# Weights of 32 experts loaded in 8 KB runs, inputs' columns permuted where they are made, the first low parts made behind the first gather, DFT tables loaded one by one

## The chip, the cores and the metric

One Trainium2 chip, one of its cores. The metric is the time of one execution in device microseconds, the median of several runs; lower is better. The profile shows one execution by engine: PE (TensorE), DVE (VectorE), ACT (ScalarE), POOL (GpSimd), SP (SyncE, which issues the DMAs of the weights).

## The reference

A backbone of two layers over 1024 tokens of 1024 columns (D), with 256 context tokens read by the first. Layer 0 mixes tokens by grouped-query attention, layer 1 by a Fourier transform; both are followed by a mixture of experts:

```python
h = _modulate(x, norm_ffn[i], sh2, sc2)          # rms norm, gain, shift, scale
lg = xt @ w_rg + b_rg                            # 4 groups of 8 experts: the best group,
le_sel = take_along_axis(xt @ w_re + b_re, ...)  # then its 2 best experts
gate = p_grp[:, None] * softmax(top_l)
# each expert e, over the tokens routed to it:
yb = (silu(xb @ w1[e]) * (xb @ w3[e])) @ w2[e]   # 1024 -> 512 -> 1024, float32
x = x + g2 * segment_sum(yb * gate)
```

w1 and w3 of an expert are 1024x512, w2 is 512x1024, all float32: 6 MiB an expert, 192 MiB a layer, each byte read once.

## The kernel before

**A MoE layer.** `phase_moe` (called once per layer) goes over the 32 experts. For each, POOL gathers up to 104 (CAP) rows of the normed input from a table H in DRAM with an indirect DMA (L1264, into one of several `xg` buffers). `xin` transposes the rows on PE and splits them into a high part `xh` (ACT) and a low part `xl` (DVE, L1277). Each weight comes in two pieces of 1 MiB, each piece as two quarters of 128x1024; `quarter` makes of a quarter its rounded part `wh` (ACT, L1203) and the rest `wl = t - wh` (DVE, L1205; one of twelve on POOL, and the first five of a layer, `POOL_FIRST`). Three matmuls per tile (L192 to L194) join them. `hidden` multiplies silu(h1) by h3 into `gg` (DVE, L1295), `gT` transposes it, and after w2 DVE scales the result by the gate (L1315), and POOL scatter-adds it to the stream Xs (L1316).

**Order of contraction.** A contraction over 1024 rows is done in 8 matmuls of 128 rows, one per partition. `load_piece` (L168 to L177) reads a piece as "(k p) n": partition p holds the rows p, 128 + p, ... of the piece, so each row is a run of its own in DRAM: 2 KB for w1 and w3, 4 KB for w2.

**Buffers.** Raw pieces go where space is free: `raw` tiles, a pair of tiles `qs`, the place of the two old row tiles (`X`, from the stage before, whole or a pair), and the tiles `wh`/`wl` of the old weights (`place`, `g.raws`). `feed` issues a load (SP queue) whenever a buffer is free. At most `NHELD` = 11 pieces of a layer are loaded before its first gather; `resume` makes SP's further loads wait until that gather has landed. `split(n)` makes the quarters ready, three ahead.

**Ahead of a layer's first gather.** The stage before (the attention's output projection in layer 0, the Fourier stage in layer 1) goes over 8 row tiles; `route_half` (L935) multiplies a tile's halves by the gain, `route_transpose` makes `hT` for the router and updates `h` (L963) for H, `route_part` picks experts and positions for some tiles (small DVE operations, L1047 to L1111). The last two tiles end the chain: `slot_index` compares positions (one-hots, L1156), PE turns them into row numbers `idx` (L1163), and POOL gathers. In layer 0 `vectors` also loads rows norm_mix, mod (`G2`, `V`) and nine tables for the DFT of the next layer, on SP, ahead of the held weights' last, and makes `V` (DVE, L1333).

Of the kernel before, what the change touches and what calls it, by code (L numbers as in the profile page):

```python
# [15 lines left out]
OP = mybir.AluOpType  # L16
# [46 lines left out]
NSP_EARLY = 3  # L63
NRAW = 3
NHELD = 11
DROP1, DROP2 = (10, (3, 4)), (27, 2)
POOL_FIRST, POOL_LAST = 5, 380
ORDER = (0, 4, 1, 5, 6, 7, 2, 3)
# [60 lines left out]


def rsqrt(g, pool, dst, src, scale, shape, tag, pw=False):
# [12 lines left out]
    nc.vector.tensor_mul(dst, dst, a)  # L144
# [22 lines left out]

def load_piece(g, src, k, eng=None):  # L168

    t = raw_tile(g)  # L170
    eng = eng or g.nc.sync
    src = src.rearrange("(k p) n -> p k n", p=P)
    ts = t if isinstance(t, list) else [t]
    k //= len(ts)
    for i, v in enumerate(ts):
        eng.dma_start(v.rearrange("p (k n) -> p k n", k=k), src[:, k * i:k * i + k])
    return t  # L177
# [622 lines left out]
def phase_wo(g):  # L800
# [4 lines left out]
    with ExitStack() as st:  # L805
# [4 lines left out]
        with ExitStack() as sw:  # L810
# [33 lines left out]
            for t in range(NT):  # L844
# [47 lines left out]
                if t == NT - 2:  # L892
                    sf.close()
                    mo.open_vectors("right")
        place(NT - 2)
        mo.open_weights("right")
        route_transpose(g, r, NT - 1, rwk, pt_)
        with tc.issue_after(r.last):
            mo.vectors()
        mo.begin_weights(r)  # L900
        route_logits(g, r, 3, rwk, pt_)
# [6 lines left out]
def route_setup(g, mo, one, wk):  # L908
# [3 lines left out]
    r.B2 = one.tile([P, D], F32, name="B2")  # L912
    nf = wk.tile([P, D], F32, name="h")
    bcast_row(g, r.A2, g.mod[l][0:1, 4 * D:5 * D])
    bcast_row(g, nf, a["norm_ffn"][l:l + 1])
    bcast_row(g, r.B2, g.mod[l][0:1, 3 * D:4 * D])
# [3 lines left out]
    nc.gpsimd.dma_start(r.W[:, :, 0:NG], a["moe_w_rg"][l].rearrange("(k p) n -> p k n", p=P))  # L920
    nc.gpsimd.dma_start(r.W[:, :, NG:NG + NE], a["moe_w_re"][l].rearrange("(k p) n -> p k n", p=P))
    r.bias = one.tile([P, NG + NE], F32, name="br")
# [32 lines left out]
def route_transpose(g, r, t, wk, pt_):  # L955
# [6 lines left out]
    transposed(g, u, r.hT[b][:, :, i], pt_, t in ACT_COPY[r.l])  # L962
    nc.vector.scalar_tensor_tensor(u, u, r.rs[t], r.B2, OP.mult, OP.add)  # L963
    r.last = nc.sync.dma_start(r.H[t * P:(t + 1) * P], u).ins
    r.order.append(t)
# [180 lines left out]
def slot_index(g, m, wk, pp, n, posm, val, tag):  # L1146
# [4 lines left out]
    for e in range(n):  # L1151
        oh = wk.tile([P, NT, CAP], BF, name="oneh")
        pe = posm(e)
# [15 lines left out]
class Moe:  # L1169


    def __init__(self, g, l):
# [11 lines left out]
        self.limit = len(self.order)  # L1184
        self.raw, self.sp = {}, {}
        self.stores = []
# [35 lines left out]
    def resume(self, ins):  # L1222

        g, n = self.g, self.nl
        self.limit = len(self.order)
        cur = g.nc.cur_bb.bb.instructions
        last = cur[-1]
        self.feed()
        for i in cur[next(k for k in range(len(cur) - 1, -1, -1) if cur[k] is last) + 1:]:
            g.tc.add_manual_dep(i, ins.name, mybir.DependencyInfo(mybir.DependencyClass.Sync, mybir.DependencyReason.DATA),  # L1230
                                reason="after the rows' gather")

    def begin_weights(self, r):
        self.limit = min(self.limit, NHELD)
        with self.g.tc.issue_after(r.last):
            self.use(4 - NRAW)
        with self.g.tc.issue_after(self.g.pow):
            self.split(NSP_EARLY - 1)

# [14 lines left out]
    def load(self, which, e, i, eng=None):  # L1254
# [35 lines left out]
    def hidden(self, h1, h3):  # L1290
# [70 lines left out]
def phase_moe(g, mo, after=None, fin=None):  # L1361
# [4 lines left out]
    with mo.st as st:  # L1366
# [26 lines left out]
        for e in range(NE + 1):  # L1393
# [29 lines left out]
            if e < NE:  # L1423
# [118 lines left out]

def dft_table(g, pool, name, tag=None):
# [4 lines left out]
    g.table = g.nc.sync.dma_start(t.bitcast(F32), src).ins  # L1548
    return t
# [513 lines left out]
```

## Time and profile before

| | us |
|---|---|
| median of 3 runs | 2396.41 |
| lowest and highest run | 2396.03, 2400.58 |
| the profiled execution, its own time | 2399.03 |
| its span, first to last instruction | 2396.9 |

The profile belongs to the execution of 2399.03 us, 2.6 above the median; 2.1 us of it lie outside the span. Over the span PE is busy 90%, DVE 80%, ACT 56% and POOL 42%, and the DMA engines move 614.22 MB. Rows of the profile give a start and a duration in us, the engine, the line of the kernel, the operation, the tile written and the tiles read.

### The profile page before, as it was taken

The numbers are of one execution on the slowest core, as the hardware profiler recorded it, in microseconds if no ns is written. First come the engines' busy times: TensorE is split into PE (matmuls) and PEld (weight loads), VectorE is DVE, ScalarE is ACT, GpSimd is POOL, SyncE is SP. The second block draws the span as 40 slices with busy tenths as digits, with TensorE's granted clock in tenths as the row PEclk, the third lists the DMA queues.
The fourth block names the chain that finished last, engine by engine and source line by source line (L and its number), as shares of the span: only waits on it lengthen the run. The fifth ranks groups of instructions, "written<-read, shape, count | busy, mean of one in ns | idle before, by whom it ended". The sixth has DMA issues, their size and how long they took to land.

```text
span 2396.9 us, 29626 instructions
## 1 busy us (share of the span) xinstructions
PE 2158.6 (90%) x10250; PEld 1427.3 (60%) x10250; DVE 1914.0 (80%) x2812; ACT 1334.2 (56%) x1741; POOL 1012.5 (42%) x562
## 2 busy tenths in 40 slices
PE   6898999999999858999999999689599999999994
PEld 3676444444445646677676667457377776666662
DVE  4868566666667897999889888666899988888895
ACT  5733433433443236777766667443387766666674
POOL 3322666666668643334333332433424433222232
PEclk8999999999999978999999999879699999999997
DMA  8544533533334769999999999745699999999996
GB/s 305 189 155 131 176 114 116 189 115 131 101 116 166 264 229 299 348 337 329 333 342 333 340 336 349 253 179 192 225 320 326 332 335 334 337 329 334 338 352 220
DMA packets 257878, 614.22 MB, mean 256 GB/s; under 512 B 26896, under 2 KB 43896, under 8 KB 251516
## 3 DMA queue, kind: packets, MB, share of 16 engines
q1 hardware_dynamic: 215676, 547.39, 65.4%
q0 software_dynamic: 24576, 54.40, 9.1%
q10 hardware_dynamic: 17472, 10.49, 1.4%
q8 instruction: 82, 1.34, 0.2%
q14 instruction: 72, 0.59, 0.1%
HBM read 559.57 MB, written 78.44 MB: 266 GB/s over the span
## 4 chain that ended last, share of the span: by engine, by line
PE 38%; DMA 29%; DVE 22%; issue 6%; ACT 3%; POOL 1%; SPq 0%; POOLq 0%; ACTq 0%; DVEq 0%
DVE wl L1205 9%; DMA raw<-in_moe_w_dram 9%; DMA wh<-in_moe_w_dram 7%; PE po L650 6%; DMA wl<-in_moe_w_dram 5%; PE sm L547 4%; PE st L644 3%; PE st L645 3%; DMA X<-in_moe_w_dram 2%; PE h L193 2%; PE h L194 2%; PE h L192 2%; PE mm L192 2%; PE mm L193 2%; PE mm L194 2%
## 5 line engine op out<-in xcount | busy, mean ns | idle before, releaser
L193 PE MATMUL h<-wl,xh 128*104 128x512 f32 x1024 | 414.5, 405 | 25.3 <-DVE wl L1205 15.0
L192 PE MATMUL h<-wh,xh 128*104 128x512 f32 x1024 | 413.5, 404 | 7.6 <-ACT wh L1203 7.5
L194 PE MATMUL h<-wh,xl 128*104 128x512 f32 x1024 | 407.7, 398 | 0.0
L670 POOL TENSOR_TENSOR acc<-acc,pe 128x1024 f32<-128x1024 f32 x125 | 298.7, 2389 | 96.5 <-ACT pe L659 94.0
L548 DVE TENSOR_REDUCE m<-sm 128x1 f32<-128x512 f32 x360 | 206.4, 592 | 136.2 <-PE sm L547 134.6
L659 ACT ACTIVATE pe<-st 128x1024 f32<-128x1024 f32 x160 | 163.9, 1025 | 261.5 <-PE st L645 258.8
L1203 ACT CAST wh<-raw 128x1024 fp32r<-128x1024 f32 x196 | 199.3, 1053 | 67.2 <-DMA raw<-in_moe_w_dram 44.3
L193 PEld LDWEIGHTS h<-wl,xh 128*104 128x104 f32 x1024 | 174.6, 171 | 103.5 <-DVE wl L1205 26.3
L1205 DVE TENSOR_TENSOR wl<-raw,wh 128x1024 fp32r<-128x1024 f32 x175 | 212.0, 1250 | 29.5 <-ACT wh L1203 28.8
L1264 POOL DMA_INDIRECT xg<-H,idx x64 | 103.5, 1617 | 302.8 <-PE pt L1275 273.4
L1203 ACT CAST wh<-wh 128x1024 fp32r<-128x1024 f32 x180 | 184.0, 1051 | 79.2 <-DMA wh<-in_moe_w_dram 48.2
L1205 DVE TENSOR_TENSOR wl<-wl,wh 128x1024 fp32r<-128x1024 f32 x163 | 205.2, 1286 | 20.3 <-ACT wh L1203 20.0
L1205 DVE TENSOR_TENSOR wl<-wh 128x1024 fp32r<-128x1024 f32 x157 | 191.8, 1246 | 33.8 <-ACT wh L1203 30.6
L192 PEld LDWEIGHTS h<-wh,xh 128*104 128x104 f32 x1024 | 174.7, 171 | 73.9 <-ACT wh L1203 13.0
L1203 ACT CAST wh<-wl 128x1024 fp32r<-128x1024 f32 x172 | 176.0, 1052 | 67.0 <-DMA wl<-in_moe_w_dram 41.3
L194 PEld LDWEIGHTS h<-wh,xl 128*104 128x104 f32 x1024 | 174.3, 170 | 59.2
L193 PE MATMUL py<-wl,gh 128*104 128x512 f32 x512 | 203.6, 398 | 0.5 <-POOL wl L1205 0.2
L194 PE MATMUL py<-wh,gl 128*104 128x512 f32 x512 | 201.2, 395 | 0.7 <-DVE gl L1306 0.7
L192 PE MATMUL py<-wh,gh 128*104 128x512 f32 x512 | 197.1, 402 | 2.0 <-ACT gh L1305 1.8
L650 PE MATMUL po<-pe,V 128*64 128x512 f32 x640 | 174.6, 624 | 0.4 <-ACT pe L659 0.4
L1316 POOL DMA_INDIRECT Xs<-y,idx x64 | 148.9, 2326 | 39.2 <-DVE y L1315 12.1
L1203 ACT CAST wh<-X 128x1024 fp32r<-128x1024 f32 x124 | 129.0, 1054 | 47.1 <-PE h L194 32.4
(569 smaller groups left out, 4496.0 us busy)
## 6 DMA issues: line engine op xcount, KB each, us to landing
raw<-in_moe_w_dram SPq DMA_DIRECT2D x98, 1024.0 KB
wh<-in_moe_w_dram SPq DMA_DIRECT2D x90, 1024.0 KB
wl<-in_moe_w_dram SPq DMA_DIRECT2D x86, 1024.0 KB
qs<-in_moe_w_dram SPq DMA_DIRECT2D x96, 512.0 KB
raw<-in_w_mod_dram SPq DMA_DIRECT2D x43, 1024.0 KB
X<-in_moe_w_dram SPq DMA_DIRECT2D x37, 1024.0 KB
X<-in_moe_w_dram SPq DMA_DIRECT2D x50, 512.0 KB
QS<-qst ACTq DMA_DIRECT2D x32, 256.0 KB
```

The lines of the kernel that those rows point to most:

```text
L192: nc.tensor.matmul(out, lh, wh, start=start, stop=False)
L193: nc.tensor.matmul(out, lh, wl, start=False, stop=False)
L194: nc.tensor.matmul(out, ll, wh, start=False, stop=stop)
L547: nc.tensor.matmul(ps[:, :kn], qs[:, h, qt * P:(qt + 1) * P], g.KS[:, g4, k0:k0 + kn], start=True, stop=True)
L548: nc.vector.reduce_max(m3[:, h, qt, b:b + 1], ps[:, :kn], axis=AX.X)
L650: nc.tensor.matmul(po[64 * h:64 * h + 64], g.V[:, kt, g4 * HD:(g4 + 1) * HD], pe[:, h], start=(kt == 0), stop=(kt == NTA - 1))
L659: nc.scalar.activation(pe, ps, AF.Exp, scale=SCALE)
L670: eng.tensor_add(acc, acc, pe)
L1203: nc.scalar.copy(h, t)
L1205: i = (nc.gpsimd if pool else nc.vector).tensor_sub(l, t, h)
L1264: self.last = self.g.nc.gpsimd.indirect_dma_start(out=xg, out_offset=None, in_=self.H if src is None else src, in_offset=bass.IndirectOffs ...
L1316: return y, lambda: nc.gpsimd.indirect_dma_start(out=self.X, out_offset=bass.IndirectOffsetOnAxis(ap=idx, axis=0), in_=y, in_offset=None, ...
```

## The change

1. A piece is read as "(p k) n": partition p holds k rows that follow each other, and a piece that goes into one tile is read in runs of 8 KB (4 KB into a pair of tiles). For the products to fit, the columns of what the weights are multiplied by are permuted: `route_half` writes `h`, and `hidden` writes `gg`, with their columns in the order in which the transposes then give them (the inner loop of the output strides 128 elements, 512 bytes). B2 is permuted by a POOL copy, the router's weights are loaded in the new order with four DMAs in place of two.
2. The first five low parts (`NLATE`) are made by DVE, after a POOL memset (`behind`) that is issued behind the first gather; the one-hots of experts 1 to 3 come after them, and the `prep` of expert 0 after X[1]. `oneh` has 3 buffers.
3. Layer 0: 2 raw buffers in place of 3, the last `place` moved, the last store of H on ACT's queue; `G2`, `V` and the product `V` move up into the loop over tiles; the nine tables load one per expert, for experts 8 to 16; G2's second row after expert 0. Layer 1's final norm comes after expert 6.

```diff
-NRAW = 3
+NRAW = (2, 3)
 NHELD = 11
 DROP1, DROP2 = (10, (3, 4)), (27, 2)
...
-def load_piece(g, src, k, eng=None):
+def load_piece(g, src, k, eng=None, order="(k p) n -> p k n"):
 
     t = raw_tile(g)
     eng = eng or g.nc.sync
-    src = src.rearrange("(k p) n -> p k n", p=P)
+    src = src.rearrange(order, p=P)
     ts = t if isinstance(t, list) else [t]
     k //= len(ts)
     for i, v in enumerate(ts):
-        eng.dma_start(v.rearrange("p (k n) -> p k n", k=k), src[:, k * i:k * i + k])
+        g.piece = eng.dma_start(v.rearrange("p (k n) -> p k n", k=k), src[:, k * i:k * i + k]).ins
     return t
 
 
...
-        place(NT - 2)
+                    mo.next_norm()
         mo.open_weights("right")
         route_transpose(g, r, NT - 1, rwk, pt_)
-        with tc.issue_after(r.last):
-            mo.vectors()
-        mo.begin_weights(r)
+        mo.begin_weights(r, lambda: place(NT - 2))
         route_logits(g, r, 3, rwk, pt_)
         with tc.issue_after(g.lt):
             mo.split(NSP - 1)
...
+def by_weights(t):
+
+    return t.rearrange("t (q j p) -> t q p j", q=2, j=4)
+
+
 def route_half(g, r, t, x1, n, wk):
 
     if n == 0:
         r.u[t] = wk.tile([P, D], F32, name="h")
     ns = slice(n * 512, n * 512 + 512)
-    g.nc.vector.tensor_mul(r.u[t][:, ns], x1[:, ns], r.A2[:, ns])
+    x, a2 = (v[:, ns].rearrange("t (p j) -> t p j", j=4) for v in (x1, r.A2))
+    g.nc.vector.tensor_mul(by_weights(r.u[t])[:, n], x, a2)
 
 
 def route_stats(g, r, t, x1, wk, junk):
...
-        pool = self.ns < POOL_FIRST if self.ns < 12 else self.ns % 12 == 9 and (self.ns < POOL_LAST or not self.l)
+        if self.ns < NLATE:
+            self.late.append((l, t, h))
+            return h, l
...
+    def finish_late(self):
+
+        for l, t, h in self.late:
+            self.vsub = self.g.nc.vector.tensor_sub(l, t, h).ins
+        self.late = []
+        self.feed()
+
...
-        nc.vector.tensor_mul(gg, s_, h3)
+
+        nc.vector.tensor_mul(gg.rearrange("t (i j p) -> t i p j", i=2, j=2), s_.rearrange("t (i p j) -> t i p j", i=2, j=2),
+                             h3.rearrange("t (i p j) -> t i p j", i=2, j=2))
...
+    def next_norm(self):
+
         g, nc = self.g, self.g.nc
         if self.l:
-            bcast_row(g, self.V, g.a["final_norm"].rearrange("(o d) -> o d", o=1), nc.sync)
-        else:
-            bcast_row(g, self.G2, g.a["norm_mix"][1:2], nc.sync)
-            bcast_row(g, self.V, g.mod[1][0:1, D:2 * D], nc.sync)
-            nc.vector.scalar_tensor_tensor(self.V, self.V, 1.0, self.G2, OP.add, OP.mult)
-            t = self.tab = {}
-            for n in ("cch", "ccl", "csh", "csl", "ce", "ci", "ca", "alt", "c0"):
-                t[n] = dft_table(g, self.vec, n)
-        bcast_row(g, self.G2, g.mod[self.l][0:1, 5 * D:6 * D], nc.sync)
+            with g.tc.issue_after(self.piece):
+                bcast_row(g, self.V, g.a["final_norm"].rearrange("(o d) -> o d", o=1), nc.sync)
+            return
+        bcast_row(g, self.G2, g.a["norm_mix"][1:2], nc.sync)
+        bcast_row(g, self.V, g.mod[1][0:1, D:2 * D], nc.sync)
+        nc.vector.scalar_tensor_tensor(self.V, self.V, 1.0, self.G2, OP.add, OP.mult)
+        self.tab = {}
+
+    def table(self, n):
+        with self.g.tc.issue_after(self.piece):
+            self.tab[n] = dft_table(self.g, self.vec, n)
 
...
-        mo.resume(mo.last.ins)
-        for t in xgs[1:]:
-            nc.gpsimd.memset(t, 0.0)
-        with tc.issue_after(g.idx):
+        first = mo.last.ins
+        with tc.issue_after(first):
+            free = nc.gpsimd.memset(mo.wk.tile([P, 1], F32, name="behind", bufs=1), 0.0).ins
+            for t in xgs[1:]:
+                nc.gpsimd.memset(t, 0.0)
+        with behind(g, free, mybir.EngineType.DVE):
+            mo.finish_late()
             prep(1, 3)
+        mo.resume(first)
...
+                if e == 0:
+                    with tc.issue_after(mo.vsub):
+                        prep(IB)
...
-                if e == 0 and mo.l:
+                if e == 0:
                     mo.vectors()
+                if e == 6 and mo.l:
+                    mo.next_norm()
+                if not mo.l and 8 <= e < 8 + len(TABLES):
+                    mo.table(TABLES[e - 8])
```

DVE, layer 0, around the first gather, before (`oneh` are the one-hots, `idx` the row numbers, `posb` the tokens' positions):

```order
L1156 TENSOR_TENSOR oneh<-jrow,posb 128x624
L1156 TENSOR_TENSOR oneh<-jrow,posb 128x208
L1161 TENSOR_SCALAR row_7460<-pi 104x1
L1163 TENSOR_TENSOR idx_7462<-row_7460,pi 104x1
L1165 TENSOR_REDUCE gate_7464<-pi 104x1
L1156 TENSOR_TENSOR oneh<-jrow,posb 128x832 x2
L1333 SCALAR_TENSOR_TENSOR V<-V,G_7178 128x1024
L1156 TENSOR_TENSOR oneh<-jrow,posb 128x832 x2
L1161 TENSOR_SCALAR row_7506<-pi 104x3
L1277 TENSOR_TENSOR xl<-pt,xh 128x416
```

and after:

```order
L1177 TENSOR_TENSOR oneh<-jrow,posb 128x624
L1177 TENSOR_TENSOR oneh<-jrow,posb 128x208
L1182 TENSOR_SCALAR row_7440<-pi 104x1
L1184 TENSOR_TENSOR idx_7442<-row_7440,pi 104x1
L1186 TENSOR_REDUCE gate_7444<-pi 104x1
L1239 TENSOR_TENSOR wl<-raw,wh 128x1024 x4
L1239 TENSOR_TENSOR wl<-X,wh 128x1024
L1177 TENSOR_TENSOR oneh<-jrow,posb 128x832 x3
L1306 TENSOR_TENSOR xl<-pt,xh 128x416
```

Five low parts stand between the first row numbers and the one-hots of the next experts; the `V` product is gone from here to the last `route_part`.

POOL, layer 0, the stretch with the first gather (`xg`), before:

```order
L1205 TENSOR_TENSOR wl<-raw,wh 128x1024 x4
L1205 TENSOR_TENSOR wl<-X,wh 128x1024
L1369 MEMSET xg 104x1024
L1384 MEMSET xg 104x1024
L1264 DMA xg<-H_61,idx_7462 104x1024
L1384 MEMSET xg 104x1024
L1264 DMA xg<-H_61,idx_7508 104x1024 x3
L1264 DMA xg<-H_61,idx_7580 104x1024 x2
```

and after:

```order
L1407 MEMSET xg 104x1024
L1293 DMA xg<-H_61,idx_7442 104x1024
L1422 MEMSET behind 128x1
L1424 MEMSET xg 104x1024 x2
L1293 DMA xg<-H_61,idx_7491 104x1024 x3
L1293 DMA xg<-H_61,idx_7617 104x1024 x2
```

The five subtractions ahead of the gather are gone, and the memset `behind` stands right after it.

SP's queue, layer 0, from the last store of a row tile on, before:

```order
L942 DMA Xs_63<-X 128x1024
L964 DMA H_61<-h 128x1024
L176 DMA wh<-in_moe_w_dram 128x4x512
L176 DMA X<-in_moe_w_dram 128x2x1024
L964 DMA H_61<-h 128x1024
L249 DMA G_7178<-in_norm_mix_dram 128x1024
L249 DMA V<-mod_60 128x1024
```

(nine tables and G2's row follow, and the rest of the weights) and after:

```order
L263 DMA G_7182<-in_norm_mix_dram 128x1024
L263 DMA V<-mod_60 128x1024
L963 DMA Xs_63<-X 128x1024
L985 DMA H_61<-h 128x1024
L190 DMA wh<-in_moe_w_dram 128x2048
L190 DMA X<-in_moe_w_dram 128x2048
L190 DMA wl<-in_moe_w_dram 128x2048
L190 DMA raw<-in_moe_w_dram 128x2048 x2
L190 DMA X<-in_moe_w_dram 128x2048
```

`G2` and `V` stand ahead of the stores of X and H, the tables are no longer here, and a weight is one run of 2048 elements per partition.

## Rows read from the trace of the kernel before

**Rows 1.** The page: GB/s in 40 slices; packets, MB and share of the weights' queue:

```profile
GB/s 305 189 155 131 176 114 116 189 115 131 101 116 166 264 229 299 348 337 329 333 342 333 340 336 349 253 179 192 225 320 326 332 335 334 337 329 334 338 352 220
...
q1 hardware_dynamic: 215676, 547.39, 65.4%
```

**Rows 2.** Windows in the MoE layers: busy time of each engine, clock, DMA share, GB/s:

```profile
1019.00:1128.00 109.00, 108.47 (x542) 80.02 (x540) 107.13 (x112) 85.43 (x96) 44.10 (x19) 1.00 1.00 332
2150.00:2250.00 100.00, 92.20 (x448) 65.04 (x447) 84.63 (x96) 66.47 (x79) 28.80 (x15) 1.00 1.02 334
```

**Rows 3.** Timeline of POOL: starts of scatter-adds, experts 0, 10, 26 and layer 1's 0:

```profile
942.68 2.45 POOL L1316 DMA_INDIRECT Xs<-y,idx  x1 [0.20 <-issue]
...
1127.62 2.38 POOL L1316 DMA_INDIRECT Xs<-y,idx  x1 [0.19 <-issue]
...
1454.31 2.40 POOL L1316 DMA_INDIRECT Xs<-y,idx  x1 [0.18 <-issue]
...
1765.74 2.41 POOL L1316 DMA_INDIRECT Xs<-y,idx  x1 [0.20 <-issue]
```

**Rows 4.** Timeline of DVE: the last low parts of layer 0 and of layer 1:

```profile
1526.98 3.39 DVE L1205 TENSOR_TENSOR wl<-wl,wh 128x1024 fp32r<-128x1024 f32 x2
...
2355.59 2.35 DVE L1205 TENSOR_TENSOR wl<-raw,wh 128x1024 fp32r<-128x1024 f32 x2
```

**Rows 5.** Timeline of POOL ahead of layer 0's first gather:

```profile
873.82 9.98 POOL L1205 TENSOR_TENSOR wl<-raw,wh 128x1024 fp32r<-128x1024 f32 x4 [0.56 <-ACT wh L1203]
883.75 2.36 POOL L1205 TENSOR_TENSOR wl<-X,wh 128x1024 fp32r<-128x1024 f32 x1
...
896.63 5.06 POOL L1264 DMA_INDIRECT xg<-H,idx  x1 [5.24 <-DMA talt<-tab_alt]
```

**Rows 6.** Timeline of DVE in the same stretch:

```profile
873.37 1.28 DVE L963 SCALAR_TENSOR_TENSOR h<-h,rs,B 128x1024 f32<-128x1024 f32 x1
874.56 2.39 DVE L1107 TENSOR_TENSOR x<-x 128x64 f32<-128x64 f32 x1
...
883.92 3.27 DVE L963 SCALAR_TENSOR_TENSOR h<-h,rs,B 128x1024 f32<-128x1024 f32 x1
...
895.60 0.15 DVE L1163 TENSOR_TENSOR idx<-row,pi 104x1 int32<-104x1 f32 x1
...
897.61 1.22 DVE L1333 SCALAR_TENSOR_TENSOR V<-V,G 128x1024 f32<-128x1024 f32 x1
```

**Rows 7.** Timeline of PE: first transposes of gathered rows, layer 0 and layer 1:

```profile
907.95 1.13 PE L1275 MATMUL pt<-ident,xg 104*128 104x104 f32 x5 [9.34 <-DMA xg<-H,idx]
...
1728.99 1.65 PE L1275 MATMUL pt<-ident,xg 104*128 104x104 f32 x8 [2.48 <-DMA xg<-H,idx]
```

**Rows 8.** Timeline of DVE ahead of layer 1's first gather:

```profile
1704.81 3.45 DVE L963 SCALAR_TENSOR_TENSOR h<-h,rs,B 128x1024 f32<-128x1024 f32 x1
...
1710.65 2.12 DVE L1098 TENSOR_TENSOR w<-w,pg 128x2 f32<-128x2 f32 x1
...
1722.46 0.15 DVE L1163 TENSOR_TENSOR idx<-row,pi 104x1 int32<-104x1 f32 x1
```

**Rows 9.** DMA in 10–20, 45–49, 1200–1440 us: packets, MB, share of 16 engines:

```profile
q1 hardware_dynamic: 654, 4.19, 101.0%
...
q1 hardware_dynamic: 806, 1.61, 105.3%
...
q1 hardware_dynamic: 31748, 74.86, 89.5%
```

**Rows 10.** Groups of DVE by line and shape: busy us, mean ns of one:

```profile
L1295 DVE TENSOR_TENSOR gg<-s,h 104x512 f32<-104x512 f32 x64 | 43.3, 677 | 2.1 <-PE h L194 2.0
...
L1621 DVE COPY add<-u 128x8 f32<-128x8 f32 x8 | 1.2, 156 | 0.0
```

**Rows 11.** Timeline of DVE in the routing of layer 0: a dense and a strided write:

```profile
892.94 0.23 DVE L1109 TENSOR_TENSOR aoh<-aoh,val 128x64 f32<-128x64 f32 x1
...
893.49 0.34 DVE L1111 TENSOR_TENSOR val<-aoh,val 128x64 bf16<-128x64 f32 x1
```

More of the change, by code (lines that the diff above doesn't have):

```diff
@@ L1 @@
 import math
-from contextlib import ExitStack, nullcontext
+from contextlib import ExitStack, contextmanager, nullcontext
 import numpy as np
@@ L63 @@
 NSP_EARLY = 3
-NRAW = 3
+NRAW = (2, 3)
 NHELD = 11
 DROP1, DROP2 = (10, (3, 4)), (27, 2)
-POOL_FIRST, POOL_LAST = 5, 380
+NLATE, POOL_LAST = 5, 380
+TABLES = ("cch", "ccl", "csh", "csl", "ce", "ci", "ca", "alt", "c0")
 ORDER = (0, 4, 1, 5, 6, 7, 2, 3)
@@ L128, in pool, with behind @@
         return st.enter_context(self.tc.tile_pool(name=name, bufs=bufs, reuse_waits="tile", **kw))
+@contextmanager
+def behind(g, ins, engine=mybir.EngineType.SP):
+    cur = g.nc.cur_bb.bb.instructions
+    last = cur[-1]
+    yield
+    for i in cur[next(k for k in range(len(cur) - 1, -1, -1) if cur[k] is last) + 1:]:
+        if i.engine == engine:
+            g.tc.add_manual_dep(i, ins.name, mybir.DependencyInfo(mybir.DependencyClass.Sync, mybir.DependencyReason.DATA),
+                                reason="behind")
 def rsqrt(g, pool, dst, src, scale, shape, tag, pw=False):
@@ L912, in route_setup @@
     r.B2 = one.tile([P, D], F32, name="B2")
-    nf = wk.tile([P, D], F32, name="h")
+    nf, b2 = (wk.tile([P, D], F32, name="h") for _ in range(2))
     bcast_row(g, r.A2, g.mod[l][0:1, 4 * D:5 * D])
+    bcast_row(g, b2, g.mod[l][0:1, 3 * D:4 * D])
     bcast_row(g, nf, a["norm_ffn"][l:l + 1])
-    bcast_row(g, r.B2, g.mod[l][0:1, 3 * D:4 * D])
+    nc.gpsimd.tensor_copy(by_weights(r.B2), b2.rearrange("t (q p j) -> t q p j", q=2, j=4))
     r.gain = lambda: nc.vector.scalar_tensor_tensor(r.A2, r.A2, 1.0, nf, OP.add, OP.mult)
@@ L919, in route_setup @@
     nc.gpsimd.memset(r.W, 0.0)
-    nc.gpsimd.dma_start(r.W[:, :, 0:NG], a["moe_w_rg"][l].rearrange("(k p) n -> p k n", p=P))
-    nc.gpsimd.dma_start(r.W[:, :, NG:NG + NE], a["moe_w_re"][l].rearrange("(k p) n -> p k n", p=P))
+    for q in range(2):
+        for nm, n0, n1 in (("rg", 0, NG), ("re", NG, NG + NE)):
+            nc.gpsimd.dma_start(r.W[:, 4 * q:4 * q + 4, n0:n1],
+                                a["moe_w_" + nm][l, q * 512:q * 512 + 512].rearrange("(p j) n -> p j n", j=4))
     r.bias = one.tile([P, NG + NE], F32, name="br")
@@ L962, in route_transpose @@
     transposed(g, u, r.hT[b][:, :, i], pt_, t in ACT_COPY[r.l])
-    nc.vector.scalar_tensor_tensor(u, u, r.rs[t], r.B2, OP.mult, OP.add)
-    r.last = nc.sync.dma_start(r.H[t * P:(t + 1) * P], u).ins
+    r.h = nc.vector.scalar_tensor_tensor(u, u, r.rs[t], r.B2, OP.mult, OP.add).ins
+    r.last = (nc.sync if r.l or t < NT - 1 else nc.scalar).dma_start(r.H[t * P:(t + 1) * P], u).ins
     r.order.append(t)
@@ L1151, in slot_index @@
     for e in range(n):
-        oh = wk.tile([P, NT, CAP], BF, name="oneh")
+        oh = wk.tile([P, NT, CAP], BF, name="oneh", bufs=3)
         pe = posm(e)
@@ L1184, in __init__ @@
         self.limit = len(self.order)
-        self.raw, self.sp = {}, {}
+        self.raw, self.sp, self.late = {}, {}, []
         self.stores = []
@@ L1192, in feed @@
     def feed(self, eng=None):
-        while self.nl < min(self.ns // 2 + self.nraw, self.limit):
+        while self.nl < min((self.ns - len(self.late)) // 2 + self.nraw, self.limit):
             self.raw[self.nl] = self.load(*self.order[self.nl], eng)
@@ L1203, in quarter @@
         nc.scalar.copy(h, t)
-        pool = self.ns < POOL_FIRST if self.ns < 12 else self.ns % 12 == 9 and (self.ns < POOL_LAST or not self.l)
+        if self.ns < NLATE:
+            self.late.append((l, t, h))
+            return h, l
+        pool = self.ns > 11 and self.ns % 12 == 9 and (self.ns < POOL_LAST or not self.l)
         i = (nc.gpsimd if pool else nc.vector).tensor_sub(l, t, h)
@@ L1222, in resume, with begin_weights @@
     def resume(self, ins):
-        g, n = self.g, self.nl
         self.limit = len(self.order)
[L1226 to L1233, printed above, removed]
-        self.limit = min(self.limit, NHELD)
[L1235 to L1238, printed above, removed]
+        with behind(self.g, ins):
+            self.feed()
+    def begin_weights(self, r, last=None):
+        self.limit = min(self.limit, NHELD)
+        with behind(self.g, r.h) if last else self.g.tc.issue_after(r.last):
+            if last:
+                last()
+            self.use(4 - NRAW[self.l])
+        self.split(NSP_EARLY - 1)
     def split(self, n):
@@ L1260, in load @@
             src = src.rearrange("o r n -> (o r) n")
-        return load_piece(self.g, src, n // P, eng)
+        t = load_piece(self.g, src, n // P, eng, "(p k) n -> p k n")
+        self.piece = self.g.piece
+        return t
     def gather(self, xg, idx, src=None):
@@ L1325, in vectors @@
     def vectors(self):
+        with self.g.tc.issue_after(self.piece):
+            bcast_row(self.g, self.G2, self.g.mod[self.l][0:1, 5 * D:6 * D], self.g.nc.sync)
+    def next_norm(self):
         g, nc = self.g, self.g.nc
         if self.l:
-            bcast_row(g, self.V, g.a["final_norm"].rearrange("(o d) -> o d", o=1), nc.sync)
-        else:
-            bcast_row(g, self.G2, g.a["norm_mix"][1:2], nc.sync)
-            bcast_row(g, self.V, g.mod[1][0:1, D:2 * D], nc.sync)
-            nc.vector.scalar_tensor_tensor(self.V, self.V, 1.0, self.G2, OP.add, OP.mult)
-            t = self.tab = {}
-            for n in ("cch", "ccl", "csh", "csl", "ce", "ci", "ca", "alt", "c0"):
-                t[n] = dft_table(g, self.vec, n)
-        bcast_row(g, self.G2, g.mod[self.l][0:1, 5 * D:6 * D], nc.sync)
+            with g.tc.issue_after(self.piece):
[6 more added lines that the diff above has]
+    def table(self, n):
+        with self.g.tc.issue_after(self.piece):
+            self.tab[n] = dft_table(self.g, self.vec, n)
     def begin(self):
@@ L1352, in open_weights @@
         g.raws[:0] = [Place(lambda n=n: g.wowA.tile([P, 2048], F32, name=n)) for n in ("wh", "wl", "wh", "wl")]
-        self.use(NRAW)
+        self.use(NRAW[self.l])
     def use(self, n):
@@ L1398, in phase_moe @@
                 mo.drop(DROP2[1], lambda b: True)
-            if e < NE:
+            if 0 < e < NE:
                 if e % IB == 0 and e + IB < NE:
@@ L1540, in phase_moe, with dft_table @@
     return state
-def dft_table(g, pool, name, tag=None):
+def dft_table(g, pool, name, tag=None, eng=None):
     src = g.tab[name]
@@ L1547, in dft_table @@
     t = pool.tile(list(src.shape), F32R, name=tag or "t" + name)
-    g.table = g.nc.sync.dma_start(t.bitcast(F32), src).ins
+    g.table = (eng or g.nc.sync).dma_start(t.bitcast(F32), src).ins
     return t
```

## The prediction

> **What bounds the kernel now.** I began with the page. In the 40 slices of the span, two stretches (slices 16 to 24 and 29 to 38) move 325 to 352 GB/s [rows 1]: the two MoE layers, some 600 us each. Then the windows inside them. In 1019–1128 us VectorE (DVE) is busy 107.13 of 109 us with the DMA share at 1.00; in 2150–2250, late in the second layer, 84.63 of 100 with the DMA share at 1.02 [rows 2]. So each MoE layer starts bound by DVE while a stock of early pieces lasts, and goes on bound by the weights' transfers. The starts of the scatter-adds give the pace: in layer 0 from expert 0 to expert 10 184.9 us, of which some 4 are an extra piece of routing (`route_extra`) that comes once, so 18.1 an expert; from expert 10 to expert 26 326.7 us, 20.4 an expert [rows 3]. The transfers are full in both parts, so what they save adds up over the whole layer, and DVE's pace, which I take as 18.2, is the floor below it.
>
> The time of a layer can be read from its last split of a weight: 1526.98 + about 2.4 = 1529.4 us in layer 0, 2355.59 + 2.3 = 2357.9 in layer 1 [rows 4] (the first row's pair shows 3.39 with a wait inside). What follows it is not edited.
>
> **Start of layer 0.** Before the first gather GpSimd (POOL) makes the low parts of five quarters, 9.98 us for four and 2.36 for the fifth [rows 5]. Beside them DVE's small routing operations take 2.2 to 2.4 us each, which otherwise take 0.15 to 0.25 ([rows 11] has one), and one `h` update 3.27 instead of the 1.28 it had just before [rows 6]. Four such small ones (the first stands in the rows) lose 8.4 us and the `h` 2.0; less 0.7 that lay in waits this is 9.7 us on the way to the indices at 895.60. Against that the `V` product (1.22 us [rows 6]) moves ahead of the routing, onto DVE's path. Indices: −8.5 us. From them to the first transposed row it takes 12.35 us (895.60 to 907.95); in layer 1, 6.5 (1722.46 to 1728.99) [rows 6 to 8]. In layer 0 the gather's issue itself takes 5.06 us [rows 5], with 1.95-us one-hot pairs and the `V` product running on DVE beside it, and nine tables just issued. The change puts nothing of DVE beside it: DVE waits for a POOL memset behind the gather's issue. I take 6.5 as in layer 1, so the landing, which also releases the weight loads, comes 8.5 + 5.9 = **14.4 us** earlier. If the wait for the issue stays, it is 8.5.
>
> What DVE then has to do: five low parts of 1.13 us and three one-hots of 1.05, 8.8 us, behind the memset; of the 5.5 to 6.5 us to the landing the first part hides, and 2 to 3 us do not. Behind them in DVE's row stands the first `xl`, which PE's first matmul waits for. I charge 2.0 us in layer 0, where the one-hots stood there before too, and 3.3 in layer 1, so DVE's own chain gains 12.4 and 5.5 us.
>
> **Start of layer 1.** Four DVE operations beside POOL's row of three low parts take 2.2, 3.45, 2.3 and 2.12 us (the second and the last stand in [rows 8]) where the second, an `h` update, alone takes 1.28 [rows 6] and the others some 0.17: 8.3 lost, with an earlier one of 1.6 partly so. I take **8.8 us** (bounds 8.3 and 9.9). [...]
>
> **8 KB runs.** In 10–20 us, loads of w_mod with long packets take 101.0% of 16 engines for 4.19 MB: 38.6 ns per KB (1,000 bytes). In 45–49 us 2 KB packets take 105.3% for 1.61 MB: 41.9. In the MoE window the weights' queue needs 89.5% of 240 us for 74.86 MB: 45.9, with scatter and gather beside it [rows 9]. The difference of the first two is 3.3 ns per KB; spread over a packet each 2 KB instead of each 8, that is 9 ns a packet, and scaled by 45.9 over about 41 (the mixture of 2 and 4 KB), 10. A whole piece of w1 or w3 goes from 512 packets to 128, 384 × 10 / 16 = 0.24 us; one of w2 from 256 to 128, 0.08. A piece in a pair of tiles gets 4 KB runs: 0.16 for w1 and w3, nothing for w2. Of 192 pieces a layer about 155 are whole, 37 in pairs; 181 come after the first gather: (155 × 0.187 + 37 × 0.107) × 181/192 = 31 us; I take **30 us a layer**. Bounds: nothing, if what limits 338 GB/s is not the packet but the other traffic, and 8% of 600 us, some 45, if the MoE's rate follows the ratio of the first two windows. The nearest rows are the two that differ in packet size alone, so I stay by them.
> [...]
>
> **Strided writes.** `gg` (64 times, 0.677 us [rows 10]) and the `h` product now write each element 512 bytes from the last. The nearest rows: a copy of 8 elements with that very stride, 156 ns [rows 10], no more than the 0.15 to 0.25 of other small ones; and `val` with a stride of 10 bytes, 0.34 us where 64 dense elements take 0.23 [rows 11], 0.11 us on 64 elements, so 0.9 on 512. Bounds 0 and 0.9 us each; I take 0, the row with the same stride and type. [...]
>
> **Tables and vectors.** Nine tables and G2 leave the start and come one an expert at 8 to 16, as small transfers beside weights, 1 to 2 us in sum; NRAW 2 changes only when early pieces start, which the first gather holds at 11 anyway. The extra `B2` copy and two more router loads lie under attention.
>
> **Sum.** Layer 0, last split. By the transfers: 1529.4 − 14.4 − 30 = 1485.0. By DVE: the first scatter at 942.68 − 12.4, then 29 experts of 18.2, 4 for the one extra routing, and about 20.6 for the last fourteen quarters with their other work: 930.3 + 552.4 = 1482.7. Two limits so close cost more than either: plus 4 (one shortage of a piece at DVE's fastest part, with the tables' 2). 1489: **−40.4**. Layer 1: by the transfers 2357.9 − 8.8 − 30 = 2319.1; by DVE 1765.74 − 5.5 + 552.4 = 2312.6 [rows 3]; plus 4: 2323.1: **−34.8**. Together −75.2 on the profiled execution's 2399.03 us: 2323.8. The median of the runs is 2396.41, 2.6 lower: I predict **2322 us**.
>
> **Rivals.**
> A, the stride costs (chance 0.19). 0.6 us on a DVE operation of 0.68 adds 19 us to DVE's limit in each layer, and 2 in the last tiles ahead: layer 0 ends at about 1505 and layer 1 at 2335, a gain of 47: **2349 us**. For: the `val` row. Against: the copy of 8.
> B, the transfers get no faster (0.10). Then the starts alone remain, 14.4 + 8.8 = 23: **2373 us**. For: DMA stays at 338 GB/s wherever it is full, and the windows of [rows 2] differ little. Against: 419 GB/s at 10 us.
> C, the transfers gain 45 a layer (0.09). DVE's limit ends it, at 1484 and 2314 with little interplay: **2307 us**.
> D, slower (0.07). The stride's price is above the bound: from 1.17 us an operation (1482.7 + 40 × 1.17 = 1529.4, with eight `h` products on the path beside 32 `gg`) layer 0 is no faster, from 1.41 layer 1 no faster; between these the sum turns. At 1.7 us, 2.4 for a `gg`, it gives 22 + 9 more: **2427 us**. DVE would be the bound in every expert.
> E, the change doesn't do what it says (0.04): the queue may split 8 KB runs into packets as before, and the waits of POOL and DVE may only change places: within 5 us of 2396.
>
> The forecast holds 0.51, its own range 2308 to 2338. The range for 8 in 10 takes in A, C and most of the way to B: 2298 to 2368. 0.2%, 4.8 us, is about what a measurement can tell from no change here: faster 0.89, within it 0.04, slower 0.07.
>
> **What would show it.** Packets of q1 fall from 215,676 [rows 1] to under 90,000 and the slices of the MoE rise to about 350 GB/s. No POOL subtraction stands ahead of the first gather and no small DVE operation there takes 2 us; the gather of layer 0 is issued in 1 to 2 us and lands near 893.5. `gg` and the `h` product keep 0.68; scatter-adds come 18 to 19.5 us apart all the way, with DVE at 95% or more of its time. The prediction is wrong if `gg` is above 1 us, if the pace from expert 10 on stays at 20, or if five low parts on DVE bring their own wait ahead of the first `xl`.

## The result, and the profile after

The changed kernel takes 2366.82 us (median of 4, 2366.0 to 2367.95) against 2396.31 in the same comparison: a ratio of 0.9873, 95% interval 0.9856 to 0.9890. That is some 30 us less; 75 were forecast. On the axis of the profile layer 0's last splits of a weight end at 1515 us and layer 1's at 2324, 14 and 34 us earlier than in [rows 4]: 14 us came from layer 0 and 20 from layer 1, where 40 and 35 were forecast. (A second profile of the same kernel, a_again below, splits them 23 and 19: its first experts start earlier.)

The page of the changed kernel, GB/s in 40 slices and the weights' queue (packets, MB, share):

```profile
GB/s 304 186 160 141 165 112 134 180 112 134 115 114 129 255 250 267 359 361 331 353 345 343 362 361 336 213 192 213 218 307 348 339 343 351 354 345 347 348 366 198
...
q1 hardware_dynamic: 110188, 546.87, 63.4%
```

Half the packets are gone: 105,488 fewer, as many as the prediction's count of pieces gives (105,200). Its sign of "under 90,000" had left out some 52,000 packets of the queue's other loads. The slices inside the MoE layers (16 to 24 and 30 to 38) carry 331 to 366 GB/s where [rows 1] has 326 to 352. Its windows, as in [rows 2] (PE, PEld, DVE, ACT, POOL busy, clock, DMA share, GB/s):

```profile
1019.00:1128.00 109.00, 107.31 (x530) 78.87 (x529) 108.53 (x112) 84.32 (x95) 45.40 (x18) 1.00 0.97 343
2150.00:2250.00 100.00, 95.27 (x444) 68.25 (x443) 91.94 (x91) 68.98 (x83) 40.12 (x16) 1.00 0.99 349
```

DVE is now fuller in both, 108.53 of 109 and 91.94 of 100. The reader should also look at the first column, which I passed over in [rows 2]: PE is at 107.31 of 109 there, and was at 108.47 before.

The starts. POOL ahead of layer 0's experts (start, duration): a new row early in the stage, the first gather, and the first scatter-add, which answers to [rows 3]:

```profile
745.64 3.98 POOL L929 COPY B<-h 128x1024 f32<-128x1024 f32 x1 [2.77 <-DMA h<-mod]
...
894.39 1.12 POOL L1293 DMA_INDIRECT xg<-H,idx  x1 [14.19 <-DVE gate L1186]
...
940.77 2.46 POOL L1347 DMA_INDIRECT Xs<-y,idx  x1 [0.18 <-issue]
```

and PE's first transposes in the two layers, and the second gather's in layer 0:

```profile
899.33 1.62 PE L1304 MATMUL pt<-ident,xg 104*128 104x104 f32 x8 [6.20 <-DMA xg<-H,idx]
...
911.66 0.91 PE L1304 MATMUL pt<-ident,xg 104*128 104x104 f32 x8 [1.54 <-DMA xg<-H,idx]
...
1708.99 1.65 PE L1304 MATMUL pt<-ident,xg 104*128 104x104 f32 x8 [6.06 <-DMA xg<-H,idx]
```

The issue takes 1.12 us in place of 5.06, and from `idx` (893.36) to the transposes it is 6.0 us: both as predicted. But the rows land only 8.6 us earlier than in [rows 7], and the first scatter-add comes 1.9 us earlier, not 12.4 (in a_again's profile 9.6, of which 2.8 are an attention that ended earlier). The scatter-adds of experts 0, 10 and 26 stand at 940.77, 1129.54 and 1437.71: 18.9 us an expert at first (18.5 before), then 19.3 (20.4 before).

The groups of DVE that write with the stride, by line (busy us, mean ns):

```profile
L1325 DVE TENSOR_TENSOR gg<-s,h 104x512 f32<-104x512 f32 x64 | 69.4, 1085 | 3.0 <-PE h L208 2.9
...
L956 DVE TENSOR_TENSOR h<-X,A 128x512 f32<-128x512 f32 x32 | 41.2, 1323 | 6.4 <-DMA H<-h 5.2 <-POOL X L1911 1.0
```

`gg` was 677 ns in [rows 10]: 0.41 us more, inside the bounds of 0 and 0.9 and not at the 0 that I took. A `gg` above 1 us was one of the prediction's own signs of being wrong; a pace of 20 from expert 10 on was another, and did not come.

### The profile page after: what moved, and what is told of

It reads as the page before. It is cut to its first block, busy times and chain, and to the rows that moved or that the text cites. A ratio compares the mean times of both kernels' runs of the same rounds, so it can differ in the third digit from the quotient of the medians.

```text
span 2364.7 us, 29621 instructions
## 1 busy us (share of the span) xinstructions
PE 2149.3 (91%) x10250; PEld 1424.5 (60%) x10250; DVE 1949.1 (82%) x2822; ACT 1338.1 (57%) x1741; POOL 1045.2 (44%) x560
## 5 line engine op out<-in xcount | busy, mean ns | idle before, releaser
L562 DVE TENSOR_REDUCE m<-sm 128x1 f32<-128x512 f32 x360 | 206.3, 591 | 136.4 <-PE sm L561 134.7
L1293 POOL DMA_INDIRECT xg<-H,idx x64 | 116.4, 1819 | 290.8 <-PE pt L1304 182.9
L1229 DVE TENSOR_TENSOR wl<-wh 128x1024 fp32r<-128x1024 f32 x157 | 206.3, 1336 | 11.7 <-ACT wh L1224 11.4
L1347 POOL DMA_INDIRECT Xs<-y,idx x64 | 178.0, 2781 | 70.3 <-DVE y L1346 29.3
```

Of the source, the lines that this page charges most:

```text
L562: nc.vector.reduce_max(m3[:, h, qt, b:b + 1], ps[:, :kn], axis=AX.X)
L1293: self.last = self.g.nc.gpsimd.indirect_dma_start(out=xg, out_offset=None, in_=self.H if src is None else src, in_offset=bass.IndirectOffs ...
L1347: return y, lambda: nc.gpsimd.indirect_dma_start(out=self.X, out_offset=bass.IndirectOffsetOnAxis(ap=idx, axis=0), in_=y, in_offset=None, ...
```

## The experiments

All are edits of the changed kernel but b_gg; the kernel before ran beside each on the same chip, and the ratios are to it.

**The first part undone, and the permuting alone undone.** a_no_runs takes the loads, `h`, `gg`, B2 and the router's weights back; a_no_perm leaves the loads:

```diff
-    x, a2 = (v[:, ns].rearrange("t (p j) -> t p j", j=4) for v in (x1, r.A2))
-    g.nc.vector.tensor_mul(by_weights(r.u[t])[:, n], x, a2)
+    g.nc.vector.tensor_mul(r.u[t][:, ns], x1[:, ns], r.A2[:, ns])
...
+        nc.vector.tensor_mul(gg, s_, h3)
...
-    nc.gpsimd.tensor_copy(by_weights(r.B2), ...)
+    bcast_row(g, r.B2, g.mod[l][0:1, 3 * D:4 * D])
# a_no_runs alone:
-        t = load_piece(self.g, src, n // P, eng, "(p k) n -> p k n")
+        t = load_piece(self.g, src, n // P, eng)
```

> The changed kernel with its 8 KB runs, late low parts and moved tables, but nothing permuted: h and gg are written densely, B2 and the router's weights are loaded as before (the weights' rows then meet the wrong columns, so the experts' products are left out as results; the work is the same). Theory 1 (the permuting eats the transfers' gain: 0.41 us on each gg puts DVE at the bound, and the B2 copy holds POOL back by 6 us ahead of layer 0's first tile): gg back to 0.68 us, DVE's pace back to 17.7 and 19.7 with slot_index, the first scatter of layer 0 some 6 to 8 us earlier, about 13 us less in each MoE layer: 2330 us, between 2322 and 2340. Theory 2 (the transfers did not get 30 us a layer faster, the stride is hidden): only the copy's 6 us come back, 2360 us or more.

> The changed kernel with the whole first part undone: the weights' rows, h, gg, B2 and the router's weights as before, the late low parts and moved tables stay. Theory 1: the start of layer 0 gains what the copy took, first scatter about 8 us earlier than the kernel before, 9 us in layer 1, the layers' pace that of before: 2378 us, between 2372 and 2384. Theory 2 expects nearly the same, 2375; the difference between this run and the one without permuting is what the transfers alone give: 50 us or more by theory 1, 15 to 20 by theory 2.

Measured: a_no_perm 2355.36 us, 0.9813 (0.9788 to 0.9838); a_no_runs 2385.98, 0.9935 (0.9913 to 0.9957). The late low parts and the moved tables are worth some 16 us, the 8 KB runs some 30 on top for both layers together, and the permuting takes about 12 to 14 back. Theory 1 (2322 to 2340) is missed, and theory 2 (2360 or more) by less. In the two profiles the stretch from the first scatter-add to that of expert 30 takes 570.5 us without permuting and 588.9 with the old rows in layer 0, 564.4 and 582.4 in layer 1: 18 us a layer, with all the work of DVE and PE in place. That the transfers gained 60 us and the permuting ate them, which was my first story, is wrong.

**The transfers by themselves.** Both kernels of this pair leave out the low parts (`quarter` makes only `wh`, and a tile is two matmuls), so that DVE and PE have time to spare; they differ in the order of the rows alone.

```diff
-        h, l = (self.hp.tile([P, 1024], F32R, name=n) for n in ("wh", "wl"))
-        nc.scalar.copy(h, t)
+        h = self.hp.tile([P, 1024], F32R, name="wh")
+        self.sub = self.vsub = nc.scalar.copy(h, t).ins
+        return h, h
...
-            mm3(self.g.nc, out, x[0][:, k], x[1][:, k], hv[:, j], lv[:, j], k == 0, k == 4 * kpp - 1)
+            self.g.nc.tensor.matmul(out, x[0][:, k], hv[:, j], start=k == 0, stop=False)
+            self.g.nc.tensor.matmul(out, x[1][:, k], hv[:, j], start=False, stop=k == 4 * kpp - 1)
```

> The kernel without permuting and with 8 KB runs, which also leaves out the low parts of the weights (no subtraction on DVE or POOL, and two matmuls per tile in place of three), so that in the MoE layers nothing but the transfers can bind. To be read against the next run, the same with the old rows. Theory 1 (each 1 MiB piece is 0.15 to 0.24 us cheaper, as predicted; in the changed kernel DVE and PE, both nearly full, keep it from being seen): from the first scatter to that of expert 30 the two differ by 26 to 31 us in each layer, and by 52 to 62 us in all. Theory 2 (the transfers themselves gain only the 18 us a layer that the runs with and without the old rows differed by): 34 to 40 us in all.

> The partner of the last run: low parts of the weights left out, rows of the weights as before the change (2 and 4 KB). Both theories: scatter-adds 19.5 to 20.2 us apart, the pace of the transfers in the kernel before, and a DMA share of 1.0; the difference to the last run decides.

Measured: 2335.68 us (0.9714, 0.9686 to 0.9742) and 2367.43 (0.9855, 0.9827 to 0.9882), 32 us apart. From the first scatter-add to that of expert 30 it is 570.2 against 586.6 us in layer 0 and 559.8 against 577.5 in layer 1: 16 and 18 us a layer. That is just short of theory 2's 34 to 40 in all and far from theory 1's 52. The four scatter-adds with 8 KB runs:

```profile
928.84 1.68 POOL L1334 DMA_INDIRECT Xs<-y,idx  x1 [3.65 <-DVE y L1333]
...
1499.01 1.60 POOL L1334 DMA_INDIRECT Xs<-y,idx  x1 [22.12 <-DVE y L1333]
...
1720.14 1.65 POOL L1334 DMA_INDIRECT Xs<-y,idx  x1 [3.61 <-DMA X<-in_moe_w_dram]
...
2279.95 1.60 POOL L1334 DMA_INDIRECT Xs<-y,idx  x1 [9.95 <-DMA Xs<-y,idx]
```

and with the old rows:

```profile
927.11 1.68 POOL L1334 DMA_INDIRECT Xs<-y,idx  x1 [3.60 <-DVE y L1333]
...
1513.73 1.60 POOL L1334 DMA_INDIRECT Xs<-y,idx  x1 [19.08 <-DVE y L1333]
...
1731.98 1.65 POOL L1334 DMA_INDIRECT Xs<-y,idx  x1 [4.48 <-DMA X<-in_moe_w_dram]
...
2309.48 1.60 POOL L1334 DMA_INDIRECT Xs<-y,idx  x1 [9.10 <-DVE y L1333]
```

A window of layer 0 in each, first with 8 KB runs and then with the old rows:

```profile
1130.00:1440.00 310.00, 221.61 (x953) 139.47 (x952) 60.34 (x96) 215.64 (x255) 40.54 (x30) 0.96 0.98 347
```

```profile
1130.00:1440.00 310.00, 222.16 (x918) 139.81 (x919) 58.14 (x92) 207.76 (x245) 42.10 (x31) 0.93 1.01 338
```

DVE is busy 60 us of 310 and PE 222, so neither binds. The long runs carry 347 GB/s in this window against 338, 2.7% more; in 905–1130 it is 344 against 330, in 2000–2200 (layer 1) 350 against 337, 4.2 and 3.8%. In time the stretches are 2.8 and 3.1% shorter. In 1130–1440 the changed kernel itself carries 350 GB/s and the kernel before 337, so the fuller DVE and PE do not keep the gain from being seen. The share falls from 1.01 to 0.98 between the two rows. In [rows 9] it was 105.3% for the 2 KB packets: there the packets' recorded times add up to more than 16 engines had in the window, so some of them overlap, and I had counted them as engine time.

**Where the permuting costs.** a_w2_old leaves `gg` dense and reads w2 as before; a_b2_act puts the copy of B2 on ACT.

```diff
# a_w2_old
+        nc.vector.tensor_mul(gg, s_, h3)
+        t = load_piece(self.g, src, n // P, eng, "(k p) n -> p k n" if which == 2 else "(p k) n -> p k n")
# a_b2_act
-    nc.gpsimd.tensor_copy(by_weights(r.B2), ...)
+    nc.scalar.copy(by_weights(r.B2), ...)
```

> The changed kernel with w2's pieces read in rows of 4 KB as before and gg written densely; w1, w3, h and B2 stay as changed. Theory 1: DVE gets back 0.41 us an expert, 13 us a layer where DVE sets the pace; w2's transfers take 0.08 us more a piece, 5 us a layer where they set it: 2350 us, between 2342 and 2357. Theory 2 (transfers bound, gg hidden): 2367 to 2376.

> The changed kernel with the permuting copy of B2 on ACT instead of POOL. Theory 1: POOL's queue loses the copy's 4 us and its wait of 2.8, the router's weights and Fourier's first products come some 5 us earlier, and with them the first gather of layer 0: 2361 us, 4 to 7 less than the changed kernel. Theory 2 (POOL has slack there, the 6 us late start has another cause such as the strided h): 2366, no change.

Measured: a_w2_old 2366.23 us, 0.9849 (0.9818 to 0.9880); a_b2_act 2368.34, 0.9857 (0.9836 to 0.9879). Neither can be told from the changed kernel, though the executions of a_w2_old lie between 2355 and 2374 us, so that it says little. Moving the copy to another engine gives nothing: from the end of attention (POOL's last sum of `acc`) to the last row statistic (`rs`) it is 142.0 us there, 139.7 in the changed kernel, 135.9 in a_no_perm.

> The kernel before with one thing of the change alone: gg is written with the stride of 512 bytes (its columns then meet the wrong rows of w2, so the experts' products are left out as results; the work is the same). Theory 1 (0.41 us of DVE is paid only where DVE or PE sets the pace, about the first ten experts of a layer, and hides behind the transfers after that): 4 us a layer, 6 to 10 us slower than the kernel before, and the scatter-adds 18.1 us apart to expert 10. Theory 2 (every expert pays): 24 to 28 us slower. Theory 3 (all of it hides): within 3 us.

This is the kernel before with the changed product for `gg` and nothing else. Measured: 2400.89 us, 1.0002 (0.9989 to 1.0015). Theory 3: in the kernel before, 0.4 us of DVE an expert does not show in the time. It is paid at first (most gaps between the first ten scatter-adds are 18.06 us, 17.74 before) and won back behind the transfers later: to the scatter-add of expert 30 it is 587.7 against 585.7 us in layer 0 and 576.3 against 580.5 in layer 1.

> The changed kernel once more, beside the three that follow: all theories expect 0.987 of the kernel before, within half a per cent.

> The changed kernel with h written densely and unpermuted (the columns of the gathered rows then meet the wrong rows of the weights, so the experts' products are left out as results; the work is the same); gg, B2 and the router's weights stay as changed. Theory 1 (of the permuting's price ahead of the MoE layers, the 0.41 us on each of 32 h products is most): the stage from the end of attention to the first gather gets 3 to 4 us shorter in layer 0 and 1 to 2 in layer 1, 2361 us against 2366. Theory 2 (the copy of B2 and the router's four loads on POOL are most): no more than 1 us in the stage, 2365.

Measured: a_again 2365.49 us, 0.9861 (0.9839 to 0.9883). a_no_h 2448.89, 1.0193 (1.0174 to 1.0211), and inconclusive: with the router's weights permuted and `h` not, other experts are chosen, one gets more rows than its tile holds, and the kernel makes extra passes (66 `gg` products in place of 64). Its stage to `rs` was 135.9 us, with the copy still in it.

> The kernel with 8 KB runs and nothing permuted once more, as the base of the two that follow (the experts' products are left out as results): 0.981 of the kernel before, as in the first run.

> The last kernel with one thing added: gg is written with the stride of 512 bytes. Theory 1 (with the transfers 16 to 18 us a layer faster and the stock of pieces larger, DVE's 0.41 us an expert is no longer hidden as it was in the kernel before): 6 to 10 us slower than the base. Theory 2 (it hides here, too, and the price of permuting lies ahead of the MoE layers): within 3 us of the base.

> The base with another thing added: POOL's strided copy of B2 ahead of the router's loads (here from and to the same columns, so that the routing stays right). Theory 1 (the copy costs little, the strided h is what made the stage ahead of layer 0's experts 3 to 4 us longer): within 2 us of the base, the stage from the end of attention to the last row statistic at 136 us. Theory 2 (the copy is the price): 4 to 6 us slower, the stage at 140.

Each adds one thing to a_no_perm: the strided product, or this line (and the load of `b2`):

```diff
+    nc.gpsimd.tensor_copy(by_weights(r.B2), by_weights(b2))
```

Measured: the base 2357.12 us, 0.9809 (0.9793 to 0.9826); a_gg 2362.54, 0.9831 (0.9814 to 0.9849); a_copy 2359.26, 0.9822 (0.9806 to 0.9838). So `gg`'s stride is worth about 5 us now, at the edge of the intervals; the copy's 2 us lie inside them. Theory 1 of a_gg falls just short of its lower bound. a_copy agrees with its theory 1 in the time and with theory 2 in the stage to `rs`, which is 140.5 us with the copy, 135.9 without.

**Better ways to permute.** a_dense turns the two DVE loops round, so that the output is dense and the inputs are strided; a_pe_perm lets PE's transposes read with a stride and permutes nothing else; a_mix takes PE for the rows and the turned loop for `gg`.

```diff
# a_dense (and gg in a_mix)
-        nc.vector.tensor_mul(gg.rearrange("t (i j p) -> t i p j", i=2, j=2), s_.rearrange("t (i p j) -> t i p j", i=2, j=2), ...
+        nc.vector.tensor_mul(gg.rearrange("t (i j p) -> t i j p", i=2, j=2), s_.rearrange("t (i p j) -> t i j p", i=2, j=2), ...
# a_pe_perm and a_mix
-                nc.tensor.transpose(pt[:, j], xg[:, (4 * q + j) * P:(4 * q + j + 1) * P], ...)
+                nc.tensor.transpose(pt[:, j], xg[:, q * 512:q * 512 + 512].rearrange("t (p j) -> t j p", j=4)[:, j], ...)
```

> The changed kernel with the loops of gg and h turned round: the output is written densely and the inputs are read with strides of 8 bytes (gg) and 16 bytes (h). Theory 1 (what costs 0.41 us is the write to another place 512 bytes on for every element): gg back at about 0.68 us and h at 0.69, some 10 us less than the changed kernel in all: 2352 to 2360. Theory 2 (any stride costs on DVE, read or written): gg stays at 1.0 us or more, 2362 to 2370.

> 8 KB runs with nothing permuted on DVE, ACT or POOL: h, gg, B2 and the router's weights as in the kernel before, and the transposes on PE read the gathered rows and gg with a stride (16 and 8 bytes), which puts the columns in the weights' order. Theory 1 (a strided read costs PE nothing): eight transposes of rows stay at 0.88 us, and the time is that of the kernel without permuting, 2350 to 2357. Theory 2 (PE pays, too): the eight take 1.5 us or more, and with PE at 96 to 97% busy a layer grows by 10 us or more: 2370 or slower.

> 8 KB runs with h, B2 and the router's weights as before the change, PE's transposes of the gathered rows read with a stride of 16 bytes, and gg written densely on DVE from inputs read with a stride of 8 bytes. Theory 1 (an 8-byte stride is free on DVE, a 16-byte one costs PE 0.3 us for eight transposes, and the four of gg are dense again): between the kernel without permuting and the one with all of it on PE: 2354 to 2358, 8 to 12 us less than the changed kernel. Theory 2 (PE's cost decides the pace): 2360 or more.

Measured: a_dense 2364.53 us, 0.9839 (0.9814 to 0.9863); a_pe_perm 2358.07, 0.9825 (0.9799 to 0.9851); a_mix 2355.87, 0.9811 (0.9792 to 0.9829). In a_pe_perm eight transposes take 1.09 us in place of 0.88, between its two theories, and the time is that of the kernel without permuting. a_mix, its theory 1, is faster than the changed kernel, whose ratio beside it was 0.9861 with an interval that does not touch this one: as fast as with nothing permuted. The lines of a_dense (ns min, median, max):

```profile
L956 DVE TENSOR_TENSOR h<-X,A x32: 1050/1086/4447, 755.6 to 1685.6; 128x512 f32<-128x512 f32 x32
...
L1325 DVE TENSOR_TENSOR gg<-s,h x64: 671/676/690, 923.0 to 2320.4; 104x512 f32<-104x512 f32 x64
```

the same lines in the changed kernel:

```profile
L956 DVE TENSOR_TENSOR h<-X,A x32: 1032/1098/2884, 757.2 to 1685.8; 128x512 f32<-128x512 f32 x32
...
L1325 DVE TENSOR_TENSOR gg<-s,h x64: 1043/1087/1130, 924.5 to 2320.5; 104x512 f32<-104x512 f32 x64
```

and PE's transposes of the rows in a_pe_perm, where the dense ones take 252:

```profile
L1300 PE MATMUL pt<-ident,xg x512: 252/283/447, 891.6 to 2275.0; 104*128 104x104 f32 x171
```

Both theories of a_dense hold, each for one product: inputs 8 bytes apart cost DVE nothing (676 ns, as dense in the kernel before; of `gg`'s two inputs `s` lies in SBUF and `h3` in PSUM), inputs 16 bytes apart as much as an output 512 bytes apart (1086 and 1098, where dense ones took 686). Its time is theory 2's: with `gg` dense again the strided `h`, the copy and the extra loads still hold some 6 us (0.9839 against 0.9813 and 0.9809), no more than the intervals.

## Why the prediction was wrong

The direction and the three mechanisms were right; four terms of the sum were not, the last of them only in how it divides over the layers. Of the 45 us missed, 26 to 31 lie in the transfers, 12 to 14 in the permuting, which stood at nothing, and 7 in the starts.

**The transfers, 30 us a layer: the main step that failed.** They gain 16 and 18 (the light pair); the runs with and without the old rows agree, 18 a layer in their profiles and 0.9935 to 0.9813 in time, some 30 us for both layers. The step was the price per KB, 38.6 against 41.9 ns, made with the shares of [rows 9]. Those windows' rates, 419 and 401 GB/s, stand in the same answers and say 4.5% for 2 KB against 8; the shares of 101.0 and 105.3% made 8.5% of it. By the rates a KB takes 38.2 and 39.9 ns of an engine, and the prediction's own working then gives 16 us a layer, about what was measured. Rival B looked at the right place, but the transfers did get faster.

**The strided write at 0 us.** It is 0.41 us on `gg` and on `h` (medians 1087 and 1098 ns against 676 and 686). The copy of 8 elements that I took as the nearest row was too short to show it; the row with the 10-byte stride erred upward. For the time this is some 5 us for `gg` by a_gg, and by a_dense some 6 for `h`, the copy and the loads together. Rival A's mechanism held at two thirds of its size, but its place did not: it was to add DVE's 19 us in each layer to the limit, and most hides behind the transfers, in the kernel before within 3 us all of it (b_gg). On DVE inputs 8 bytes apart took 676 ns, inputs 16 bytes apart 1086 and outputs 512 bytes apart 1098; why the first is free here and the other two cost the same, no run shows. On PE the weight loads that read the stride take 214 ns at 8 bytes and 218 at 16, against 140.

**"The extra `B2` copy and two more router loads lie under attention."** They don't. The copy waits 2.77 us for its row and takes 3.98 in POOL's queue, ahead of the router's loads; PE idles 1.97 us for the copy and 0.61 for the last of the loads. In the stage to `rs` it is 139.7 us in the changed kernel (137.8 in a_again, 138.3 to 142.6 in the three others with `h` and B2 permuted), 135.5 to 137.9 in the eight changed kernels with nothing permuted there, and 133.8 before (136.4 in b_gg, with the same stage). The copy alone makes 140.5 (a_copy), `h` dense with the copy kept 135.9 (a_no_h). With profiles of the same stage 2 to 3 us apart, the permuting costs it some 4 us, and how these divide between the copy and the strided `h` stays open. Putting the copy on ACT did not help, so it is not POOL's queue alone.

**"2 to 3 us do not" hide behind the landing.** From the first transposes to the first scatter-add of layer 0 it was 34.7 us before, and is 38.2 to 39.2 in ten of the runs with late low parts: 3.5 to 4.5, where 2.0 were charged, with the five low parts on DVE ahead of the second gather's row numbers. In the profile of the changed kernel it is 41.4, with PE idle 1.54 us before the second transposes and the granted clock at 0.50 in 915–920; a_again, with no such idle time and the clock at 1.00 in 910–920, has 38.4. In layer 1 it was 36.8 and is 38.3 to 39.5 in most runs, 1.5 to 2.7 where 3.3 were charged, so over both layers this term came out near its 5.3.

What held: no subtraction on POOL ahead of a gather; `rs` to `idx` 14.7 us in place of 23.0 in layer 0, 8.3 less (8.5 forecast), and 16.2 in place of 25.8 in layer 1, 9.6 less (8.8 forecast); 6.0 us from `idx` to the rows. In a_no_runs the first scatter-add comes 11.6 us earlier, of which 2.0 are an attention that ended earlier in that profile; the sum had 12.4. In all it is some 16 us faster and not 23: the weights are released 15 us earlier (892.72 in place of 907.95), but in the 5-us windows from 895 on its DMA shares are 0.98, 0.46, 1.02 and 0.80, against 1.03, 0.91 and 0.99 from 910 on before. That the buffers are not free earlier is my reading of it and was not tried by itself.

What the sum had left out: PE. At 108.47 of 109 us in [rows 2] it was as full as DVE, so the floor of 18 us an expert that I gave to DVE alone was that of both. Two runs bear on it. The strided `gg` adds 0.41 us to DVE alone, and most gaps among the first ten scatter-adds go from 17.74 us (a_no_perm) to 18.07 (a_gg). The strided transposes add some 0.3 us to PE alone, and the gaps go to between 17.73 and 18.15 (a_pe_perm). No run made PE's work alone lighter.

## What to carry to other kernels

Price longer DMA runs by GB/s of windows in which the queue is full, not by the share of busy time, which stood at 1.05 in [rows 9] where the recorded times of packets overlap; and test it with the compute left out. Where a layout has to be permuted, first try the reads of a pass that is made anyway (a transpose on PE, or a DVE product with inputs 8 bytes apart) before strided writes and extra copies. Test the parts one by one: here the measured ones add up (16 from the starts, 30 from the transfers, 12 to 14 back for the permuting, against 30 in all), so the forecast of 75 failed by the size of its terms and not by adding them.

## What the runs showed of the hardware

On DVE a product with inputs 8 bytes apart took 676 ns, as a dense one did (`gg`, 104x512 f32, one input in SBUF and one in PSUM; a_dense and the kernel before); one with inputs 16 bytes apart took 1086 ns (`h`, 128x512, a_dense), about as much as with an output 512 bytes apart (1098, the changed kernel), where the dense one took 686; outputs 8 bytes apart were not tried. PE's transposes that read with a stride of 16 or 8 bytes took 283 and 281 ns against 252, their weight loads 218 and 214 against 140 (a_pe_perm, against the changed kernel). Packets of 8 KB in place of 2 and 4 gave 2.7 to 4.2% of rate beside scatter and gather (the light pair: 347 GB/s against 338, 344 against 330) and 2.8 and 3.1% of the time there; long packets in place of 2 KB gave 4.5% between two stretches without them (419 GB/s against 401 in the kernel before).
